# Shifting SBUF tiles with pads so that dense float32r operands start alike modulo 256 bytes, and returning a residual in two halves

## The chip, the cores and the metric

The kernel runs on one core of one Trainium2 chip. The metric is the device time in microseconds (us) of one launch; the time of a kernel is the median of its runs. The profile is one execution on the same core, taken by the hardware profiler. A product below is one TensorE matmul instruction.

## What is computed

The reference is two model blocks over 512 tokens of width 1024, in float32, with 256 tokens of context.

- The first block normalises the tokens, multiplies them by `w_in`, runs a retention mixer and an RWKV-7 scan (both directions), multiplies by `w_out`, adds the residual, and applies a mixture of 16 experts with 64 tokens each.
- The second block has two layers. Layer 0 mixes by three groups of dilated attention (all q, k, v from one normalised input), multiplies by `a_wo`, adds the result to its input `h` (the residual), and applies an MLP. Layer 1 mixes by a gated convolution and applies a second MLP:

```python
h = h + y
h = h + mlp_sq_relu(rms_norm_2(h, norm2[i]), mlp_w1[i], mlp_w2[i])   # square(relu(x @ w1)) @ w2
```

## The kernel before, in words

**Dense products.** Every large matrix product is made of float32r products. Both operands are split into a high and a low float32r part (`split`, L156 to L159), and three products add up in PSUM: high by high, low by high, high by low. There are four places that issue them, always with 128 rows of contraction, 128 output partitions and (but for the 256 context tokens) 512 columns:

- `tok_major` (L333 to L335): tokens stationary (`hHi`, `hLo`, `cHi`, `cLo`), weights moving (`w_hi`, `w_lo`): (6+6+4) blocks of 24, 384 products.
- `mm3` (L162 to L164) from `ch_major`: weights stationary, `hHi`/`hLo` moving: 24 calls of 24, 576 products, and 240 products of 256 columns on the context. The same line from `dense_b`: weights `whi`/`wlo` stationary, `y2Hi`/`y2Lo` moving, 3 times 704 = 2112 products (the first matrix of both MLPs and the convolution's input).
- L706 to L708 (`mh`, `ml` stationary, `w_hi`, `w_lo` moving) and L1326 to L1328 (`mix` stationary, `Wo` moving): 96 products each, the two halves of `w_out`.
- `dense_g` (L1822 to L1824): activations stationary, weights `whi`/`wlo` moving: 3 times 640 products on `yHi`/`yLo` (attention projections and `a_wo`), 3 times 512 on `aHi`/`aLo` (second matrix of both MLPs) and 3 times 64 on `gHi`/`gLo` (convolution's output).

Weights come by DMA from DRAM in 512 KB pieces on SyncE's (SP's) queue (`ahead`, L1794 on), in the order of the list `plan`, and ScalarE and VectorE split them one or two pieces ahead of use.

**Where tiles lie.** SBUF tiles come from pools that are stacked from the left end or the right end of each partition in the order in which the code opens them. No row of the profile shows an address; added up from the pools' sizes, the first bytes modulo 256 are: `w_hi`, `w_lo`, `Wo`, `whi`, `wlo`, `yHi`, `yLo`: 224. `hHi`, `hLo`, `cHi`, `cLo`: 192. `mix`: 128. `mh`, `ml`: 96. `y2Hi`, `y2Lo`, `aHi`, `aLo`, `gHi`, `gLo`: 0. Slices of 128 or 512 float32 columns keep the same remainder. For attention group 1 the value projection reads `yHi` with a stride of four columns (L2043, `yHi[:, k, b::4]`), so its slices begin at 224, 228, 232 and 236. So before the change the pair of operands is alike (224 and 224) in the products on `yHi`/`yLo`, and unlike in the other dense products.

Of plain float32 products, the attention's value product `po` (L2156, L2158) has `PPT` and `v` at 224 and 224; the scan's `cV` (L1082) has `uUV` and `uL` at 224 and 224; the scan's `cU` (L1094) has `cv` at 224 and `TT` at 128.

**Around the residual.** After the first block the residual `xres` ([128, 4, 1024] float32, 2 MB) is copied to DRAM (`sx`), and its two column halves, `raws[0]` and `raws[1]`, serve as buffers for the attention's projections. For each half of the heads (`hf`) and each group (`g`), `project` makes q in `raws[0]`, k in `raws[1]` and v; a generator `qk_T` normalises, rotates and transposes q or k in small steps, run between the steps of the next dense product by `drive` from the list `jobs`; `attend` is put in the same list. With `g == 2` v is made in `raws[0]`, stored to DRAM (`sV`, L2061, one DMA for each of four blocks) and loaded back in another order (L2068, four DMAs) into a tile of its own.

At the end of the last group (`hf` 1, `g` 2) the whole residual is loaded back by one DMA (L2260) on SP's queue, behind the loads of v. Then the first half of `a_wo`'s rows is multiplied (`dense_g` with `halves=(0, 1)`) while `jobs` still runs the last attention group and the merge of the groups: first output columns 0 to 511, then columns 512 to 1023. `add_res` adds each block's PSUM sum to `xres` on VectorE (L1856) and so frees the PSUM buffer; there are four accumulators.

Of the kernel before, what the change touches and what calls it, by code (L numbers as in the profile page):

```python
# [10 lines left out]
F32 = mybir.dt.float32  # L11
# [116 lines left out]
def _body(tc, nc, st, A, out, dbg, stop):  # L128
    V, ACT, PE, POOL = nc.vector, nc.scalar, nc.tensor, nc.gpsimd
    cst = st.enter_context(tc.tile_pool(name="cst", bufs=1))  # L130
    psp = [None]

    def ps(name="ps", tag="p"):
# [38 lines left out]
    pw = pa.enter_context(ExitStack())  # L172
    wr = pw.enter_context(tc.tile_pool(name="wr", bufs=4, side="right"))
    wh = pw.enter_context(tc.tile_pool(name="wh", bufs=3, side="right"))
    hp = pw.enter_context(tc.tile_pool(name="hp", bufs=1, side="right"))
    pr_ = pa.enter_context(ExitStack())
    M = pr_.enter_context(tc.tile_pool(name="M", bufs=10))
# [21 lines left out]
    xt, raws = [], {}  # L199
# [291 lines left out]
    for i in range(4):  # L491
        for d in range(2):
            b = i if d == 0 else 3 - i
# [63 lines left out]
    for pr in range(4):  # L557
        sg = []
        for d in range(2):
            a, _ = ch_major(1536 + 512 * d + pr * 128, False)  # L560
            t, g = med([128, S], name="gt"), med([128, S], name="sg")
# [18 lines left out]
    NT = S + CT  # L580
    p1 = pa.enter_context(ExitStack())
    P1 = p1.enter_context(tc.tile_pool(name="P1", bufs=1))
    W3 = p1.enter_context(tc.tile_pool(name="W3", bufs=1))

    def wide(name, tag="W3", bufs=3):
# [282 lines left out]
    ZX = xps.enter_context(tc.tile_pool(name="zX", bufs=3, side="right"))  # L868
    pools = {n: p2.enter_context(tc.tile_pool(name=n, bufs=4, side="right")) for n in ("uL11", "uKB", "uL12", "UP")}
    UP = pools["UP"]  # L870
    ZP, RP_, TP, LP = (p2.enter_context(tc.tile_pool(name=n, bufs=1)) for n in ("ZP", "RP", "TP", "LP"))
    mask = const("mask", nc.scalar, pool=ZP)
    anti = const("anti", nc.scalar, pool=ZP)
    epsg = ZP.tile([128, 1], F32, name="epsg")
# [855 lines left out]
    C1 = pc_.enter_context(tc.tile_pool(name="C1", bufs=1, side="right"))  # L1730
    WC = pc_.enter_context(tc.tile_pool(name="WC", bufs=3, side="right"))
    TC = pc_.enter_context(tc.tile_pool(name="TC", bufs=1))

    def tmp(shape, name, bufs, dt=F32):
        return TC.tile(shape, dt, tag=name, name=name, bufs=bufs)
# [40 lines left out]
    for l in range(2):  # L1776
        if l:
            for j in range(4):
                for i in (1, 2, 0):
                    plan += cols(Wb, i * 1024 + j * 256)  # L1780
        if l:
            for n in range(2):
                plan += rows(Wbo, 0, n * 512)
        else:
            r0, r1 = rows(Wo, 0, 0), rows(Wo, 0, 512)
            plan += r0[:2] + r1[:2] + r0[2:] + r1[2:]
        for qf in range(4):
            for j in range(4):
                plan += cols(W1[l], qf * 1024 + j * 256)
            for n in range(2):  # L1790
                plan += rows(W2[l], qf * 1024, n * 512)
# [19 lines left out]
    def dense_g(lhs, done, halves=(0, 1, 2, 3), before={}):  # L1811

        acc = [ps("acc", "a") for _ in range(4)]
        for half in halves:
            hi, lo = weights([128, 2, 512])
            if half in before:
                before[half]()
            for b in range(4):
                for kk in range(2):
                    k = half * 2 + kk  # L1820
                    xh, xl = lhs(k, b)
                    PE.matmul(acc[b], xh, hi[:, kk], start=k == 2 * halves[0], stop=False)  # L1822
                    PE.matmul(acc[b], xl, hi[:, kk], start=False, stop=False)  # L1823
                    PE.matmul(acc[b], xh, lo[:, kk], start=False, stop=k == 2 * halves[-1] + 1)  # L1824
                if half == halves[-1]:
                    done(b, acc[b])
                yield
# [19 lines left out]
    def nat(t):  # L1847
        return lambda k, b: (t[0][:, k, b * 128:(b + 1) * 128], t[1][:, k, b * 128:(b + 1) * 128])
# [112 lines left out]
    def qk_T(raw, dst, g, i):  # L1961

        sq_ = tmp([128, 4, 8], "qss", 2)
        for b in range(4):
            t = tmp([128, 512], "qsq", 2)
            ACT.activation(t, raw[:, b], AF.Square)
            V.tensor_reduce(sq_[:, b], t.rearrange("p (h d) -> p h d", d=64), axis=AX.X, op=OP.add)
            if b % 2:
                yield
        r = rsqrt(TC, sq_.rearrange("p b h -> p (b h)"), 32, EPS, 1.0 / 64)  # L1970
        yield

        def turn(b):
            x3 = raw[:, b].rearrange("p (h d) -> p h d", d=64)
            V.tensor_tensor(x3, x3, r[:, b * 8:b * 8 + 8, None].to_broadcast([128, 8, 64]), op=OP.mult)
            t = tmp([128, 8, 2, 8], "qrp", 2)
            xr = x3[:, :, 0:16].rearrange("p h (t d) -> p h t d", t=2)
            V.tensor_tensor(t, xr[:, :, ::-1], rt[:, g, i, b, 1].rearrange("p (t d) -> p t d", t=2)[:, None]
                            .to_broadcast([128, 8, 2, 8]), op=OP.mult)
            x16 = x3[:, :, 0:16]  # L1980
            V.tensor_tensor(x16, x16, rt[:, g, i, b, 0][:, None].to_broadcast([128, 8, 16]), op=OP.mult)
            V.tensor_tensor(x16, x16, t.rearrange("p h t d -> p h (t d)"), op=OP.add)

        def trans(b):
            pt = ps("pt", "t")
            for pr in range(4):
                PE.transpose(pt[:, pr * 128:(pr + 1) * 128], raw[:, b, pr * 128:(pr + 1) * 128], ident)  # L1987
            if g == 0:
                o, s_ = dst[:, :, b * 128:(b + 1) * 128], pt.rearrange("p (r t) -> p r t", r=4)
                ACT.activation(o, s_, AF.Copy, scale=gsc[:, g, i:i + 1])  # L1990
            else:
                ns = 4 if g == 1 else 16
                mm = 128 // ns
                for pr in range(4):
                    o = dst[:, pr].rearrange("p (s m) -> p m s", s=ns)[:, b * mm:(b + 1) * mm]
                    ACT.activation(o, pt[:, pr * 128:(pr + 1) * 128].rearrange("p (m s) -> p m s", s=ns), AF.Copy,
                                   scale=gsc[:, g, i:i + 1])

        for b in range(6):
            if b < 4:  # L2000
                turn(b)
            yield
            if b > 1:
                trans(b - 2)
                yield
# [3 lines left out]
    def drive(main, n=1):  # L2009

        for _ in main:
            for j in list(jobs):
                for _ in range(n):
                    if next(j, jobs) is jobs:
                        jobs.remove(j)
                        break

    def drain():
        while jobs:
            drive([0])  # L2020

    def project(hf, g):

        own = []
        dst = []
        for i in range(2):
            dst.append(AT.tile([128, 4, S], F32, name="qkT", tag=f"qk{i}", bufs=2))
            raw = raws[i]
            bf = {}
            if hf == g == i == 0:  # L2030
                bf = {0: lambda: turns(range(4), 0, y1), 1: lambda: (turns((4, 5), 0, y1), ranks()),
                      2: lambda: (turns((6, 7), 0, y1), tables())}
            drive(dense_g(nat(y1), qk_evac(raw), before=bf))
            for j in own:
                for _ in j:
                    pass
                if j in jobs:
                    jobs.remove(j)
            own = [qk_T(raw, dst[i], g, i)]
            jobs.extend(own)  # L2040
        lhs = nat((yHi, yLo))
        if g == 1:
            lhs = lambda k, b: (yHi[:, k, b::4], yLo[:, k, b::4])  # L2043
        if g == 2:
            v = raws[0]
        else:
            v = AT.tile([128, 4, 512], F32, name="v", tag="v")
        vx = None
        if g == 0:
            vx = AT.tile([128, 4, 512], F32, name="vx", tag="vx", bufs=1)  # L2050

        def done(b, acc):
            r = rr[g == 1][:, b:b + 1]
            ACT.activation(v[:, b], acc, AF.Copy, scale=r)
            if g == 0:
                if b:
                    V.tensor_scalar(vx[0:64, b - 1], acc[0:64], r[0:64], None, op0=OP.mult)
                if b < 3:
                    V.tensor_scalar(vx[64:128, b + 1], acc[64:128], r[64:128], None, op0=OP.mult)
            if g == 2:  # L2060
                nc.sync.dma_start(sV[hf, b * 128:(b + 1) * 128], v[:, b])  # L2061

        drive(dense_g(lhs, done))
        drain()
        if g == 2:
            v = AT.tile([128, 4, 512], F32, name="v", tag="v")
            for j in range(4):
                nc.sync.dma_start(v[:, j], sV[hf].rearrange("(m s) n -> s m n", s=16)[4 * j:4 * j + 4])  # L2068
        return dst[0], dst[1], v, vx

    def attend(g, O, md, qT, kT, v, vx):
# [185 lines left out]
            jobs.append(j)  # L2257
    for pr in range(4):
        split(yHi[:, pr], yLo[:, pr], oT0[:, pr])
    nc.sync.dma_start(xres, sx)  # L2260
    ss = sums()
    drive(dense_g(nat(y1), add_res(0), halves=(0, 1)), 4)
    drive(dense_g(nat(y1), add_res(1), halves=(0, 1)), 2)
    drain()
    at_.close()
    y2 = [pc_.enter_context(tc.tile_pool(name=n, bufs=1)).tile([128, 8, S], F32R, name=n) for n in ("y2Hi", "y2Lo")]
# [83 lines left out]
```

## Time and profile before

| | us |
|---|---|
| median of 3 runs | 2904.22 (2894.70 to 2904.94) |
| profiled execution, its own time | 2906.07 |
| span of its instructions | 2904.2 |
| TensorE busy | 2746.8 (95%) |
| VectorE busy | 1360.5 (47%) |
| ScalarE busy | 1024.9 (35%) |
| mean granted TensorE clock | 0.96 of full speed |

Matmuls are pipelined, and their ends are modelled: a row gives a product some 0.4 us, while the next one starts 0.23 us later. What a stream of products costs is therefore read from the distance of their starts. A row of busy time by stretch gives for each engine its busy time and, in brackets, its number of instructions, then TensorE's granted clock, the DMA engines' busy share and GB/s.

### The profile page before, as it was taken

What the parts mean: (1) busy time and instruction counts of PE and PEld (TensorE: products, weight loads), DVE (VectorE), ACT (ScalarE), POOL (GpSimd) and SP (SyncE); (2) the same over time, 40 slices, a digit from 0 to 9 for tenths busy, and PEclk for the clock granted to TensorE, in tenths of its full rate; (3) what the DMA queues carried; (4) which work ended last, traced back from release to release, by engine and by line L of the source; (5) the groups of instructions that cost most, each with busy time, mean ns of one, the idle gap of its engine ahead of it and who ended that gap; (6) DMA issues with size and microseconds to landing.
All of it is one profiled execution on the core that took longest, in us unless ns stands there. A gap on an engine that the chain in (4) does not pass through costs nothing.

```text
span 2904.2 us, 38123 instructions
## 1 busy us (share of the span) xinstructions
PE 2746.8 (95%) x15198; PEld 1951.0 (67%) x15198; DVE 1360.5 (47%) x2452; ACT 1024.9 (35%) x1988; POOL 268.2 (9%) x266
## 2 busy tenths in 40 slices
PE   7999997578899999979999999989999999999999
PEld 5767555457744444438688667857888888888887
DVE  4354286897621111236545654655344454444433
ACT  4232354356411111125446444634223332333223
POOL 1102045545100000011000000000000000000000
PEclk9999987789899999999999999988999999999999
DMA  6205755436779999983122211232222223222222
GB/s 246 81 22 170 232 176 164 145 105 168 268 283 409 408 409 409 409 307 121 51 63 91 70 59 59 66 109 66 94 94 94 94 89 94 94 93 95 93 93 92
DMA packets 253329, 456.33 MB, mean 157 GB/s; under 512 B 32367, under 2 KB 127160, under 8 KB 252640
## 3 DMA queue, kind: packets, MB, share of 16 engines
q1 hardware_dynamic: 236272, 438.44, 43.4%
q10 hardware_dynamic: 13632, 7.79, 0.9%
q0 software_dynamic: 3248, 7.67, 0.8%
q8 instruction: 120, 1.97, 0.3%
q14 instruction: 57, 0.47, 0.0%
HBM read 425.45 MB, written 28.40 MB: 156 GB/s over the span
## 4 chain that ended last, share of the span: by engine, by line
PE 72%; DVE 6%; DMA 3%; ACT 1%; issue 0%; POOL 0%; SPq 0%; DVEq 0%; ACTq 0%
PE pe L1555 11%; PE acc L1822 10%; PE acc L1824 10%; PE acc L1823 10%; PE accb L162 6%; PE accb L163 6%; PE accb L164 6%; PE pS L2104 2%; DVE zZ L973 2%; DVE zT L971 2%; DMA wexp<-in_w_down 1%; PE po L2156 1%; PE pt L1987 1%; PE pf L2233 1%; DMA xres<-sx 1%; PE pgat L1583 1%
## 5 line engine op out<-in xcount | busy, mean ns | idle before, releaser
L159 DVE TENSOR_TENSOR wlo<-wc,whi 128x1024 fp32r<-128x1024 f32 x238 | 291.4, 1224 | 483.0 <-ACT whi L158 468.5
L158 ACT CAST whi<-wc 128x1024 fp32r<-128x1024 f32 x240 | 251.8, 1050 | 499.3 <-PE acc L1823 313.7
L1822 PE MATMUL acc<-whi,yHi 128*128 128x512 f32 x640 | 274.9, 431 | 6.3 <-DVE xres L1856 5.9
L163 PE MATMUL accb<-y2Lo,whi 128*128 128x512 f32 x704 | 278.4, 395 | 0.0
L162 PE MATMUL accb<-y2Hi,whi 128*128 128x512 f32 x704 | 277.6, 395 | 0.1
L164 PE MATMUL accb<-y2Hi,wlo 128*128 128x512 f32 x704 | 277.5, 395 | 0.0
L1555 PE MATMUL pe<-wexp,xg 128*64 128x512 f32 x1008 | 263.7, 597 | 1.5 <-DMA wexp<-in_w_up 1.5
L1824 PE MATMUL acc<-wlo,yHi 128*128 128x512 f32 x640 | 258.8, 405 | 0.0
L1823 PE MATMUL acc<-whi,yLo 128*128 128x512 f32 x640 | 257.2, 402 | 0.0
L1822 PE MATMUL acc<-whi,aHi 128*128 128x512 f32 x512 | 202.7, 396 | 0.0
L1823 PE MATMUL acc<-whi,aLo 128*128 128x512 f32 x512 | 202.6, 396 | 0.0
L1824 PE MATMUL acc<-wlo,aHi 128*128 128x512 f32 x512 | 202.5, 396 | 0.0
L1555 PEld LDWEIGHTS pe<-wexp,xg 128*64 128x64 f32 x1008 | 89.2, 136 | 150.9 <-issue 144.9
L1822 PEld LDWEIGHTS acc<-whi,yHi 128*128 128x128 f32 x640 | 131.5, 206 | 43.8 <-issue 15.7
L163 PEld LDWEIGHTS accb<-y2Lo,whi 128*128 128x128 f32 x704 | 132.0, 187 | 32.6 <-DVE y2Lo L1749 0.5
L162 PEld LDWEIGHTS accb<-y2Hi,whi 128*128 128x128 f32 x704 | 131.9, 187 | 32.7 <-ACT whi L158 0.5
L164 PEld LDWEIGHTS accb<-y2Hi,wlo 128*128 128x128 f32 x704 | 132.0, 187 | 31.9
L1824 PEld LDWEIGHTS acc<-wlo,yHi 128*128 128x128 f32 x640 | 131.1, 205 | 28.9 <-issue 4.8
L1823 PEld LDWEIGHTS acc<-whi,yLo 128*128 128x128 f32 x640 | 132.2, 207 | 20.7 <-issue 1.4
L1823 PEld LDWEIGHTS acc<-whi,aLo 128*128 128x128 f32 x512 | 96.2, 188 | 23.3
L1822 PEld LDWEIGHTS acc<-whi,aHi 128*128 128x128 f32 x512 | 96.2, 188 | 23.2
L1824 PEld LDWEIGHTS acc<-wlo,aHi 128*128 128x128 f32 x512 | 96.2, 188 | 23.2
(656 smaller groups left out, 4645.1 us busy)
## 6 DMA issues: line engine op xcount, KB each, us to landing
wexp<-in_w_gate SPq DMA_DIRECT2D x64, 1024.0 KB
wc<-in_mlp_w SPq DMA_DIRECT2D x128, 512.0 KB
wexp<-in_w_up SPq DMA_DIRECT2D x62, 1024.0 KB
wexp<-in_w_down SPq DMA_DIRECT2D x62, 1024.0 KB
wc<-in_a_wqkv SPq DMA_DIRECT2D x72, 512.0 KB
wmod<-in_w_mod SPq DMA_DIRECT2D x32, 512.0 KB
w_b<-in_w_in SPq DMA_DIRECT2D x24, 512.0 KB
wc<-in_b_win SPq DMA_DIRECT2D x24, 512.0 KB
```

The costliest lines, as they stand in the source:

```text
L158: ACT.copy(hi, src)
L159: eng.tensor_tensor(lo, src, hi.bitcast(F32), op=OP.subtract)
L162: PE.matmul(o, whi, xhi, start=first, stop=False)
L163: PE.matmul(o, whi, xlo, start=False, stop=False)
L164: PE.matmul(o, wlo, xhi, start=False, stop=last)
L971: V.tensor_tensor(tm, Z[:, j + 1:, j:j + 1].to_broadcast([128, m, j]), Z[:, j:j + 1, :j].to_broadcast([128, m, j]), op=OP.mult)
L973: V.tensor_tensor(Z[:, j + 1:, :j], Z[:, j + 1:, :j], tm, op=OP.add)
L1555: PE.matmul(o[n][64 * e:64 * e + 64], lhs(k, e), w[e][:, kk, n * 512:n * 512 + 512], start=k == 0, stop=k == 7)
L1822: PE.matmul(acc[b], xh, hi[:, kk], start=k == 2 * halves[0], stop=False)
L1823: PE.matmul(acc[b], xl, hi[:, kk], start=False, stop=False)
L1824: PE.matmul(acc[b], xh, lo[:, kk], start=False, stop=k == 2 * halves[-1] + 1)
L2104: PE.matmul(pS[:, x * wd + lo:x * wd + hi], qT[r, pr, b * 128:(b + 1) * 128], kT[r, pr, ks], start=True, stop=True)
```

## The change

The change opens small pools that hold nothing but a pad (224, 128, 96 and 224 bytes per partition) at four places of the stack, so that tiles opened behind each pad move by that many bytes. On the right side `hHi`, `hLo`, `cHi`, `cLo` (with the other tiles of `hp`) go from 192 to 224. On the left `mh`, `ml` go from 96 to 224; `mix`, with the scan's tiles behind it (`TT` and others), from 128 to 224; everything that layer 0 and layer 1 open behind the pool `TC` goes up by 224, so `y2Hi`, `y2Lo`, `aHi`, `aLo`, `gHi`, `gLo` from 0 to 224, and the attention's `v` from 224 to 192. No instruction is added by a pad.

The residual comes back in eight DMAs of 256 KB in place of one of 2 MB: columns 512 to 1023 as soon as the last k has been transposed out of `raws[1]` (a generator `back(1)` chained to `qk_T`), columns 0 to 511 after the loads of v. The first half of `a_wo`'s rows is then multiplied in the other order of columns, 512 to 1023 first, and the list of weights follows.

```diff
+    def pad(stack, name, n, side="left"):
+
+        stack.enter_context(tc.tile_pool(name=name, bufs=1, side=side)).tile([128, n // 4], F32, name=name)
+
...
     wh = pw.enter_context(tc.tile_pool(name="wh", bufs=3, side="right"))
+    pad(pw, "padh", 224, "right")
     hp = pw.enter_context(tc.tile_pool(name="hp", bufs=1, side="right"))
...
     P1 = p1.enter_context(tc.tile_pool(name="P1", bufs=1))
+    pad(p1, "pad3", 128)
     W3 = p1.enter_context(tc.tile_pool(name="W3", bufs=1))
...
-    ZP, RP_, TP, LP = (p2.enter_context(tc.tile_pool(name=n, bufs=1)) for n in ("ZP", "RP", "TP", "LP"))
+    ZP = p2.enter_context(tc.tile_pool(name="ZP", bufs=1))
+    pad(p2, "padm", 96)
+    RP_, TP, LP = (p2.enter_context(tc.tile_pool(name=n, bufs=1)) for n in ("RP", "TP", "LP"))
...
     TC = pc_.enter_context(tc.tile_pool(name="TC", bufs=1))
+    pad(pc_, "padc", 224)
...
-            plan += r0[:2] + r1[:2] + r0[2:] + r1[2:]
+            plan += r1[:2] + r0[:2] + r0[2:] + r1[2:]
...
+    def back(n):
+        for b in range(4):
+            nc.sync.dma_start(raws[n][:, b], sx[:, b, n * 512:n * 512 + 512])
+        yield
...
             own = [qk_T(raw, dst[i], g, i)]
+            if hf and g == 2 and i:
+
+                own = [itertools.chain(own[0], back(1))]
             jobs.extend(own)
...
                 nc.sync.dma_start(v[:, j], sV[hf].rearrange("(m s) n -> s m n", s=16)[4 * j:4 * j + 4])
+            if hf:
+                for _ in back(0):
+                    pass
...
-    nc.sync.dma_start(xres, sx)
     ss = sums()
-    drive(dense_g(nat(y1), add_res(0), halves=(0, 1)), 4)
-    drive(dense_g(nat(y1), add_res(1), halves=(0, 1)), 2)
+    drive(dense_g(nat(y1), add_res(1), halves=(0, 1)), 4)
+    drive(dense_g(nat(y1), add_res(0), halves=(0, 1)), 2)
     drain()
```

## Rows read from the trace of the kernel before

**Rows 1.** The page, its first part: busy time of TensorE, share of span, instructions.

```profile
PE 2746.8 (95%) x15198; PEld 1951.0 (67%) x15198; DVE 1360.5 (47%) x2452; ACT 1024.9 (35%) x1988; POOL 268.2 (9%) x266
```

**Rows 2.** The chain of waits from 1976 us to the end, by line.

```profile
by line: PE accb L162 17.8%; PE accb L163 17.7%; PE accb L164 17.7%; PE acc L1823 15.1%; PE acc L1824 15.1%; PE acc L1822 15.0%; PE pt L1746 1.2%; PE prb L2299 0.1%; DVE xres L1858 0.1%; ACT qsq L1860 0.1%; issue 0.0%; ACTq L2346 0.0%; ACTq
```

**Rows 3.** Busy time by stretch: length, PE, PEld, DVE, ACT, POOL, clock, DMA, GB/s.

```profile
34.00:140.00 106.00, 104.20 (x536) 81.38 (x535) 46.17 (x83) 35.01 (x59) 12.38 (x9) 0.98 0.38 124
190.00:300.00 110.00, 108.58 (x515) 77.40 (x514) 44.42 (x63) 35.77 (x51) 22.90 (x24) 1.00 0.46 144
300.00:500.00 200.00, 179.83 (x689) 112.38 (x688) 125.59 (x121) 88.93 (x128) 68.95 (x49) 0.87 0.60 185
2040.00:2904.00 864.00, 860.15 (x3723) 691.64 (x3721) 364.01 (x437) 262.52 (x346) 0.00 (x0) 1.00 0.29 93
```

**Rows 4.** Timeline, TensorE, y2 by whi (0 and 224), 16 triples: start, duration.

```profile
2199.92 0.40 PE L162 MATMUL accb<-y2Hi,whi 128*128 128x512 f32 x1
...
2211.12 0.40 PE L162 MATMUL accb<-y2Hi,whi 128*128 128x512 f32 x1
```

**Rows 5.** Timeline, TensorE, whi by aHi (224 and 0), 7 triples.

```profile
2600.42 0.40 PE L1822 MATMUL acc<-whi,aHi 128*128 128x512 f32 x1
...
2605.32 0.40 PE L1822 MATMUL acc<-whi,aHi 128*128 128x512 f32 x1
```

**Rows 6.** Timeline, TensorE, hHi by w_hi (192 and 224), 14 triples.

```profile
224.10 0.39 PE L162 MATMUL acc<-hHi,w_hi 128*128 128x512 f32 x1
...
233.90 0.40 PE L162 MATMUL acc<-hHi,w_hi 128*128 128x512 f32 x1
```

**Rows 7.** Timeline, TensorE, whi by yHi (224 and 224), 15 triples.

```profile
1870.18 0.39 PE L1822 MATMUL acc<-whi,yHi 128*128 128x512 f32 x1
...
1880.38 0.39 PE L1822 MATMUL acc<-whi,yHi 128*128 128x512 f32 x1
```

**Rows 8.** Timeline, TensorE, whi by yHi with a stride of four columns, 7 triples.

```profile
1480.19 0.39 PE L1822 MATMUL acc<-whi,yHi 128*128 128x512 f32 x1
...
1485.12 0.40 PE L1822 MATMUL acc<-whi,yHi 128*128 128x512 f32 x1
```

**Rows 9.** Groups by line and shape: count, busy us, mean ns of one, idle before.

```profile
L1822 PE MATMUL acc<-whi,yHi 128*128 128x512 f32 x640 | 274.9, 431 | 6.3 <-DVE xres L1856 5.9 <-ACT yHi L1748 0.4
L1823 PE MATMUL acc<-whi,yLo 128*128 128x512 f32 x640 | 257.2, 402 | 0.0
L1822 PE MATMUL acc<-whi,aHi 128*128 128x512 f32 x512 | 202.7, 396 | 0.0
L1082 PE MATMUL cV<-uUV,uL 128*64 128x64 f32 x384 | 24.0, 243 | 23.6 <-ACT uUV L1072 17.3 <-DVE uUV L1074 6.0
L1094 PE MATMUL cU<-cv,TT 128*64 128x64 f32 x384 | 19.3, 239 | 0.0
```

**Rows 10.** The chain of waits, 1900 to 2050 us: start, us, what.

```profile
1901.52 20.30 DMA xres<-sx
```

**Rows 11.** Timeline around the residual; in brackets idle time and what ended it.

```profile
1904.80 1.79 PE L2156 MATMUL po<-diag,v 128*64 128x128 f32 x16 [1.99 <-DMA v<-sV]
1921.91 0.69 DVE L1856 TENSOR_TENSOR xres<-acc,xres 128x512 f32<-128x512 f32 x1 [5.83 <-DMA xres<-sx]
1922.66 0.79 PE L1822 MATMUL acc<-whi,yHi 128*128 128x512 f32 x1 [5.91 <-DVE xres L1856]
1939.07 0.69 DVE L1856 TENSOR_TENSOR xres<-acc,xres 128x512 f32<-128x512 f32 x1 [0.49 <-PE acc L1824]
```

**Rows 12.** Busy time by stretch around the residual, columns as in rows 3.

```profile
1922.00:1930.00 8.00, 7.34 (x58) 4.54 (x59) 5.86 (x14) 2.40 (x17) 0.00 (x0) 0.57 0.01 3
```

**Rows 13.** Timeline, SP's queue: storing v and loading it back.

```profile
1893.42 3.77 SPq L2061 DMA_DIRECT2D sV<-xres  x3
1899.01 2.47 SPq L2068 DMA_DIRECT2D v<-sV  x4
```

**Rows 14.** DMA view, 1900 to 2050 us: GB/s in 40 slices of 3.75 us.

```profile
GB/s 126 260 245 194 108 86 1 0 146 0 140 2 139 1 0 0 0 0 0 4 140 0 137 23 120 9 131 144 0 29 129 122 140 35 111 140 44 96 140 39
```

## The prediction

> **What bounds the kernel now.** I read the page's first part, the chain of waits, the busy time by stretch and then the timeline of single products. TensorE is busy for 95% of the span [rows 1]. From 1976 us to the end the chain of waits is nearly nothing but dense products of L162 to L164 and L1822 to L1824 [rows 2], and from 2040 to 2904 us TensorE is busy for 860.15 of 864 us at a granted clock of 1.00, with VectorE at 364, ScalarE at 263 and the DMA engines at 0.29 [rows 3]. So in the last 30% of the kernel the time is the number of products times the distance of their starts, and nothing else is near. The same holds early on: 104.20 of 106 us from 34 to 140 us, 108.58 of 110 from 190 to 300; from 300 to 500 us TensorE still has 179.83 of 200, at a clock of 0.87 [rows 3].
>
> The distance of starts is what the pads can touch, and the trace holds products of both kinds. A triple is three products on the same operands. With y2 by whi (0 and 224 modulo 256) 16 triples take 2211.12 - 2199.92 = 11.20 us, so 48 products are 233.3 ns apart [rows 4]. With whi by aHi (224 and 0) 21 products take 4.90 us: 233.3 ns [rows 5]. With hHi by w_hi (192 and 224) 42 take 9.80 us: 233.3 ns [rows 6]. With whi by yHi (224 and 224), on the very line and weights of the aHi products, 45 products take 1880.38 - 1870.18 = 10.20 us: **226.7 ns** [rows 7]. With a stride of four columns in yHi 21 products take 4.93 us, 234.8 ns [rows 8]: three of four slices are unlike there, and the stride is a second difference. All five stretches are free of other work, and one product lasts 0.39 or 0.40 us in each, so the clock is the same. The one difference between rows 5 and rows 7 that the code shows is where the tile begins. 6.6 ns of 233.3 is 2.8%.
>
> The Trainium skill (TensorE: Matmul & The Clock Gate, "Step-by-step: what each phase is for") speaks against this reading: TensorE has two separate SBUF read ports, and loading the next tile's weights takes no read bandwidth from the running matmul. By that rule the relative start of two operands would not matter, and the first rival below would be the outcome. The trace disagrees so far, with 226.7 against 233.3 ns. The same page gives some 216 ns for the distance of warm products of 512 columns, which neither kind reaches here.
>
> **The change, part by part.** The sum is made against the profiled execution's own 2906.07 us (span 2904.2 and 1.87 around it); the median of the runs, 2904.22, is 1.85 lower.
>
> *padc.* It turns y2, a and g from 0 to 224, so 2112 + 1536 + 192 = 3840 products become alike. All lie after 1976 us, where TensorE is the whole chain [rows 2, 3]. At 233.3 - 226.7 = 6.6 ns each that is 25.3 us. Bounds: nothing, if the start is not the cause; 25.3 us if every product reaches 226.7 (no stretch shows less). I take 25.3, since these products run in long streams as those of rows 7 do, but with one reserve that is a rival below: in rows 7 the tokens are stationary and the weights move, while in the 2112 products on y2 it is the other way round.
>
> *padh, pad3, padm.* 576 + 384 + 96 + 96 = 1152 products of 512 columns become alike; at 6.6 ns each, 7.6 us. TensorE bounds the first stretches and less so the third [rows 3], and short bursts between other work may not settle at 226.7. I take two thirds, 5 us; the ends are 0 and 7.6.
>
> *Plain float32 products.* padc makes `po` unlike (v goes to 192, PPT stays at 224), padm makes `cU` alike. In the scan a group that is alike (`cV`, 243 ns) and one that is not (`cU`, 239 ns) [rows 9] show no price either way, so I take nothing. Bounds: if 6.6 ns held here too, the 256 products of `po`, two instructions each, would lose 3.4 us and the 384 instructions of `cU` would gain 2.5.
>
> *The residual.* The load of 2 MB is issued at 1901.52 us and takes 20.30 us on the chain [rows 10]. VectorE stands 5.83 us for it and TensorE, which needs the accumulators, 5.91 us [rows 11]. After that pause the granted clock is 0.57 for 8 us [rows 12], between its levels of 1.2 and 2.4 GHz; against the full clock that is 0.43 x 8 = 3.4 us. Removed: up to 9.3 us.
>
> Added are seven DMA issues on SP's queue. The three stores of v there take 3.77 us in all, most of it waiting for v's blocks, and the four loads of v 2.47 us, 0.6 each [rows 13]. `back(1)` falls behind the second store, so its four issues (some 2.5 us by the loads' price) lie in those waits; behind them in the queue stand the last two stores, the weights' next piece and the loads of v, and for those waits the value product of the last group, which already stands 1.99 us for v [rows 11]. Its 1 MB also lies ahead of v on the DMA engines: at the 245 to 260 GB/s of the busiest slices [rows 14] that is an estimated 4 us. So v comes 0 to 4.3 us later, in part at a lower clock. I take 2 us, because the stores leave the engines idle for part of that time, and keep 0 and 5 as ends.
>
> `back(0)` stands behind the loads of v, in the place of the old load, with half its bytes. It is wanted only after the first 48 products on columns 512 to 1023 and the attention steps between them; before, the second set of additions began at 1939.07 us, 17.2 us after the first [rows 11], and its data would even at the old load's 20.30 us be there at about 1922 us. It is hidden; if the last rings were as late as that and the stage had come forward by 9 us, it would still not be waited for. Behind it on SP's queue is one piece of weights, which is not wanted before those additions. The swapped order of columns costs nothing, as the list of weights is swapped with it. When the stall is gone, the next late thing is the serial chain of the merge, which the change leaves alone.
>
> Residual in all: 9.3 - 2 = about 7 us, ends 4 and 9.
>
> **Sum:** 25.3 + 5 + 7 = 37.3 us; 2906.07 - 37.3 = 2868.8, and 1.85 less as the median stands: **2867 us**, 1.3% faster.
>
> **Rivals.**
>
> 1. *The start does not matter.* The 226.7 ns would come from something else in the projections, as where yHi lies as a whole. For it: only one tile pair shows the short distance. Against it: rows 5 and 7 share line, shape, weights and clock. Then only the residual counts: 2906.07 - 7 - 1.85 = 2897 us, no change that can be told. Chance 0.10. (The skill's rule on the two ports gives this time.) That the pads do not reach 224 would look the same, but the sums of bytes leave no doubt: 0 + 224, 96 + 128, 128 + 96, and 192 - 224 = 224 modulo 256.
>
> 2. *Only products with the tokens stationary gain.* The 2112 on y2 and the 576 on hHi stay at 233.3. Then 1728 x 6.6 = 11.4 us, 2 us of the token mixer and 7 of the residual: 20.4 us, so 2884 us, 0.7% faster. For it: no pair with moving tokens that is alike stands in the trace. Against it: unlike pairs cost 233.3 ns both ways round [rows 4, 5]. Chance 0.10.
>
> 3. *Alike is the dear kind, and the kernel slows.* For it: the groups' mean for one product is 402 ns on yLo against 396 on aHi, and 431 on yHi [rows 9]. If that were the cost of being alike, 3840 products would lose 6 ns each, 23 us; less the residual's 7 that is 16 us more, 2920 us. It decides from 1.8 ns a product on. Against it: ends are modelled, the groups on yHi mix in stretches of low clock and breaks by attention work, and the clean starts say the opposite [rows 7]. Chance 0.05.
>
> **How the numbers follow.** My forecast has the remaining 0.75. About 0.5% (14.5 us) is what a measurement of this kernel can tell from no change; the runs of before alone spread by 10 us. Forecast and rival 2 are faster by more than that: 0.85. Rival 1 is the same: 0.10. Rival 3 is slower: 0.05. For the range, the low end takes 25.3 + 7.6 + 9 and 2.5 of `cU`: 44 us, 2860, and I go to 2858; the high end takes in rival 2 with the residual's lower end, 2887. Rivals 1 and 3 are left out.
>
> **What would show it.** Right: in the second MLP a triple takes 0.680 us in place of 0.700, and the stretch that took 864 us takes some 840; the triples on hHi take 0.680 as well; L1856 waits for no DMA, and the clock stays up around 1920 us. Wrong: triples still 0.700 us (rival 1); 0.680 on L1822 to L1824 but 0.700 on L162 to L164 (rival 2); longer ones (rival 3); a wait of the value product for v well over 2 us, which would eat the residual's part; or a new limit in the MLPs, visible as idle time of TensorE on the split of weights.

## The result and the profile after

| | before | after |
|---|---|---|
| median | 2899.46 us (4 runs, 2891.11 to 2904.94) | 2866.03 us (4 runs, 2860.30 to 2868.56) |
| profiled execution: own time, span | 2906.07, 2904.2 us | 2863.71, 2861.6 us |
| mean granted clock | 0.960 | 0.962 |

The ratio is **0.9884 [0.9851, 0.9918]**: 1.2% faster. Where it went is read from five landmarks, the first starts of named products in the two profiled executions:

| stretch, us | before | after | difference |
|---|---|---|---|
| start to the first expert product | 815.9 | 808.3 | -7.6 |
| experts, to the first attention projection | 489.1 | 489.1 | 0 |
| attention and merge, to the first product on y2 | 688.5 | 678.7 | -9.8 |
| first MLP, to the first product on gHi | 499.5 | 485.8 | -13.7 |
| the rest (convolution, second MLP) | 411.2 | 399.8 | -11.4 |

So 25.1 of 42.6 us come from the last two rows, which only the pads can touch. The page's first part, TensorE (answers to rows 1), and the busy time of the last stretch, which is shifted by 17.4 us so that it holds the same work as the last of rows 3:

```profile
PE 2710.8 (95%) x15198; PEld 1948.4 (68%) x15198; DVE 1358.0 (47%) x2452; ACT 1025.2 (36%) x1988; POOL 269.5 (9%) x266
```

```profile
2022.60:2861.60 839.00, 835.16 (x3718) 691.04 (x3716) 363.05 (x436) 261.85 (x346) 0.00 (x0) 1.00 0.30 96
```

The number of instructions and the clock of 1.00 are as before (3718 records against 3723), VectorE's and ScalarE's work is the same, and TensorE is idle for under 4 of the 839 us. The same products stand closer together. The timeline of TensorE in the kernel after shows by how much; each pair of rows is the first and the last start of an unbroken stretch, of 540 products on y2, 189 on aHi and 42 on hHi (answers to rows 4 to 6):

```profile
2338.73 0.39 PE L167 MATMUL accb<-y2Hi,whi 128*128 128x512 f32 x1
...
2461.16 0.39 PE L167 MATMUL accb<-y2Hi,whi 128*128 128x512 f32 x1
...
2640.03 0.39 PE L1832 MATMUL acc<-whi,aHi 128*128 128x512 f32 x1
...
2682.87 0.39 PE L1832 MATMUL acc<-whi,aHi 128*128 128x512 f32 x1
...
210.81 0.40 PE L167 MATMUL acc<-hHi,w_hi 128*128 128x512 f32 x1
...
220.36 0.39 PE L167 MATMUL acc<-hHi,w_hi 128*128 128x512 f32 x1
```

(2461.16 - 2338.73) / 540 = 226.7 ns, (2682.87 - 2640.03) / 189 = 226.7, (220.36 - 210.81) / 42 = 227.4; before they were 233.3 each. The groups by line and shape say it more faintly (answers to rows 9), because a product's end is modelled:

```profile
L1832 PE MATMUL acc<-whi,yHi 128*128 128x512 f32 x640 | 272.7, 428 | 0.4 <-ACT yHi L1758 0.4
L1832 PE MATMUL acc<-whi,aHi 128*128 128x512 f32 x512 | 199.4, 389 | 0.0
L1103 PE MATMUL cU<-cv,TT 128*64 128x64 f32 x384 | 18.5, 233 | 0.1
```

aHi falls from 396 to 389 ns. The group on yHi, whose tiles the change did not touch, keeps its duration (431 and 428), but the 6.3 us of idle time in front of it, 5.9 of them for the residual, are gone.

The second part of the change shows in SP's queue (answers to rows 13), with the columns start, time to the last issue of the row, and count:

```profile
1874.09 3.55 SPq L2034 DMA_DIRECT2D xres<-sx  x2
...
1880.50 3.53 SPq L2034 DMA_DIRECT2D xres<-sx  x2
1884.08 0.43 SPq L2079 DMA_DIRECT2D sV<-xres  x1
...
1887.61 0.45 SPq L2034 DMA_DIRECT2D xres<-sx  x1
...
1889.69 0.89 SPq L2034 DMA_DIRECT2D xres<-sx  x2
...
1892.03 4.24 SPq L2086 DMA_DIRECT2D v<-sV  x4
1896.31 2.42 SPq L2034 DMA_DIRECT2D xres<-sx  x1
```

Four loads of the residual are issued before the first store of v and three more before the loads of v; only the last stands behind those, where the code puts four. No addition of the residual waits for a DMA any more. What is late next is v: the view of the tile `po` lists the waits of the value product, and the busy time by stretch gives the clock behind that wait and in an earlier stretch of the attention.

```profile
L2177 PE MATMUL po<-diag,v x64: 272/273/476, 1899.8 to 1923.3; 128*64 128x128 f32 x64
its engine sat idle before it (us, times) until:
  DMA v<-sV: 3.0, 1
```

```profile
1652.40:1666.10 13.70, 13.70 (x31) 7.78 (x30) 7.90 (x15) 1.04 (x1) 0.00 (x0) 0.51 0.12 39
1901.00:1909.00 8.00, 8.00 (x89) 4.87 (x91) 4.26 (x13) 2.21 (x12) 0.00 (x0) 0.57 0.40 126
```

TensorE waits 3.0 us where it waited 1.99 [rows 11], and then runs at 0.57 for 8 us, mostly at its lower level of 1.2 GHz. Before, it ran at the lower level for 3.4 us behind the wait for v and for 10.2 us behind the wait for the residual [rows 12]; now for 6.8 us, once.

### The profile page after: what moved, and what is told of

Its sections match the earlier page's. It is cut to its first block, busy times and chain, and to the rows that moved or that the text cites. A ratio compares the mean times of both kernels' runs of the same rounds, so it can differ in the third digit from the quotient of the medians.

```text
span 2861.6 us, 38144 instructions
## 1 busy us (share of the span) xinstructions
PE 2710.8 (95%) x15198; PEld 1948.4 (68%) x15198; DVE 1358.0 (47%) x2452; ACT 1025.2 (36%) x1988; POOL 269.5 (9%) x266
## 4 chain that ended last, share of the span: by engine, by line
PE 72%; DVE 6%; DMA 3%; ACT 1%; issue 0%; POOL 0%; SPq 0%; DVEq 0%; ACTq 0%
PE pe L1564 11%; PE acc L1832 10%; PE acc L1834 10%; PE acc L1833 10%; PE accb L167 6%; PE accb L168 6%; PE accb L169 6%; PE pS L2125 2%; DVE zT L980 2%; DVE zZ L982 2%; DMA wexp<-in_w_down 1%; PE po L2177 1%; PE pt L1997 1%; PE pf L2254 1%; PE pgat L1592 1%; PE pT L2154 1%
## 5 line engine op out<-in xcount | busy, mean ns | idle before, releaser
L163 ACT CAST whi<-wc 128x1024 fp32r<-128x1024 f32 x240 | 252.2, 1051 | 474.7 <-PE acc L1833 299.8
L1833 PEld LDWEIGHTS acc<-whi,yLo 128*128 128x128 f32 x640 | 131.0, 205 | 20.5 <-issue 1.3
```

Of the source, the lines that this page charges most:

```text
L163: ACT.copy(hi, src)
```

## The experiments

Four questions: does each half of the change give what the sum says; is it the relative start of the operands that counts, and how exactly; what made the residual early; and what the next late thing is worth.

**The halves alone.** Three kernels on one chip, in runs by turns with the kernel before (21 runs): the changed kernel (5), the pads alone (6), and the residual alone (10). The edit for the pads alone, against the changed kernel:

```diff
-            if hf and g == 2 and i:
-                own = [itertools.chain(own[0], back(1))]
...
-            if hf:
-                for _ in back(0):
-                    pass
...
+    nc.sync.dma_start(xres, sx)
-    drive(dense_g(nat(y1), add_res(1), halves=(0, 1)), 4)
-    drive(dense_g(nat(y1), add_res(0), halves=(0, 1)), 2)
+    drive(dense_g(nat(y1), add_res(0), halves=(0, 1)), 4)
+    drive(dense_g(nat(y1), add_res(1), halves=(0, 1)), 2)
```

The residual alone leaves out the four lines `pad(pw, "padh", ...)`, `pad(p1, "pad3", ...)`, `pad(p2, "padm", ...)` and `pad(pc_, "padc", ...)`.

> The changed kernel itself, as a yardstick on the same chip for its two parts. If the parts are independent, its gain is the sum of the gains of the next two runs: some 33 us off the kernel before (1.2%), 25 us of it after the first product on y2.

> Only the pads; the residual returns in one load at the old place. If the common start is the cause: every dense triple outside the attention falls from 0.700 to 0.680 us, the stretch from the first product on y2 to the end shortens by 25 us (911 to 886), the stretch up to the first expert product by 5 to 8 us, and the wait of L1856 for the residual (5.8 us) stays: about 32 us faster. If the start did nothing and the whole gain were the residual's: no change that can be told.

> Only the residual's return in halves, no pads. My theory: the wait of 5.8 us and the 10 us at the low clock behind it go, the value product waits 1 us longer for v, so 7 to 10 us between the first attention product and the first product on y2; triples in the MLP stay at 0.700 us. Rival: the low clock only comes at another place, and the gain is no more than the 5.9 us of TensorE's pause.

| | median, us | ratio to before (2897.18) | y2 to the end, us |
|---|---|---|---|
| both | 2864.32 | 0.9878 [0.9858, 0.9897] | 885.5 |
| pads | 2866.87 | 0.9897 [0.9877, 0.9917] | 885.6 |
| residual | 2890.24 | 0.9974 [0.9958, 0.9989] | 910.5 |

The parts add up: 1.03% + 0.26% = 1.29%, against 1.22%. The stretch from the first product on y2 to the end takes 910.7 us in the kernel before; the pads bring it to 885.6, the residual leaves it alone. The residual is worth 0.0026 x 2897 = 7.5 us (3 to 12 by its interval), or 5.5 by the difference of the first two runs. With the pads alone the stall is where it was; the timeline of VectorE and the chain of waits of that run:

```profile
1910.72 0.69 DVE L1866 TENSOR_TENSOR xres<-acc,xres 128x512 f32<-128x512 f32 x1 [4.63 <-DMA xres<-sx]
```

```profile
1890.56 20.06 DMA xres<-sx
```

In the residual's own run the wait for v and the lower clock behind it grew; the timeline of TensorE shows the value product:

```profile
1902.43 1.97 PE L2173 MATMUL po<-diag,v 128*64 128x128 f32 x16 [4.14 <-DMA v<-sV]
```

Here the clock stands at the lower level from 1901.1 to 1911.4 us. So the rival named for this run, that the low clock only comes at another place and no more than 5.9 us is gained, holds in its first half for this execution, and a gain of 3 to 12 us does not rule out the second.

One more thing is read from these runs. In 11 of the 14 profiled executions the clock falls to the lower level for 13.7 us (17.1 in one) some 355 us into the attention; in the residual's run it does not (same stretch, counted from the first projection):

```profile
1659.80:1673.50 13.70, 13.59 (x58) 8.65 (x57) 12.45 (x27) 1.93 (x3) 0.00 (x0) 1.00 0.14 39
```

Nothing in the code differs there. From the first product of the first merge (`pf`, some 347 us into the attention) to the start of the wait for v, the three executions without it take 246.4 us, and five that have it and also load the residual in eight take 252.2 or 252.3. So such a stretch is worth some 6 us, and it comes and goes between executions; the stretch at the merge is another (30.7 us in the profiled execution of before, 23.9 in two others, 17.1 to 20.5 in the rest, among them the pads alone). Of the 9.8 us between projections and y2, then, the 4.7 in the merge can't be put down to the change, and one profile can't settle a question of 5 us about this part of the kernel; medians of many runs can.

**The relative start.** Three kernels with other pads follow, each run once; the one run of before beside them took 2904.24 us. First, whole multiples of 32 bytes off:

```diff
-    pad(pc_, "padc", 224)
+    pad(pc_, "padc", 32)
...
+        pad(pm_, f"pada{i}", (32, 128)[i])
...
+    pad(cv_, "padg", 64)
```

> Pads changed so that the activations stand otherwise to the weights (which stay at 224 modulo 256): y2 64 bytes on, a of the first MLP 96, g 128, a of the second MLP 192. If only equality modulo 256 helps, all four are 0.700 us a triple and the end is 25 us later than in the changed kernel. If a smaller modulus were enough (64 or 128), y2, g and the second a stay at 0.680 us. If the kernel before merely stood at a bad distance of 32 bytes, all four are at 0.680 us or below.

2873.35 us, span 2871.2. The timeline of TensorE in this run, stretches of 540 products on y2 (start of activation less start of weight: 64 modulo 256), 189 on aHi in the first MLP (96) and 141 on gHi (128):

```profile
2342.71 0.39 PE L167 MATMUL accb<-y2Hi,whi 128*128 128x512 f32 x1
...
2466.31 0.39 PE L167 MATMUL accb<-y2Hi,whi 128*128 128x512 f32 x1
...
2018.69 0.39 PE L1832 MATMUL acc<-whi,aHi 128*128 128x512 f32 x1
...
2062.96 0.40 PE L1832 MATMUL acc<-whi,aHi 128*128 128x512 f32 x1
...
2467.00 0.39 PE L1832 MATMUL acc<-whi,gHi 128*128 128x512 f32 x1
...
2499.76 0.39 PE L1832 MATMUL acc<-whi,gHi 128*128 128x512 f32 x1
```

228.9, 234.2 and 232.3 ns; aHi in the second MLP (192) stands at 228.8. So the price is graded: differences of 64 and 192 cost 2.2 ns a product, 128 some 5.6, 96 and the 32 of before 6.6 to 7.5. None of the three outcomes named ahead of the run came out. The stretch from y2 to the end takes 898.6 us, 13.1 longer than with equal starts (885.5) and 12.1 shorter than before: a price that is all or nothing would have given the whole 25. Then, small differences:

```diff
+        pad(pm_, f"pada{i}", 192)
...
+            o = (1, 8)[i]
+            aHi, aLo = (AP_.tile([128, 8 * S + 64], F32R, name=n)[:, o:o + 8 * S].rearrange("p (k n) -> p k n", k=8)
+                        for n in ("aHi", "aLo"))
...
+    y2 = [pc_.enter_context(tc.tile_pool(name=n, bufs=1)).tile([128, 8 * S + 8], F32R, name=n)[:, 4:4 + 8 * S]
+          .rearrange("p (k n) -> p k n", k=8) for n in ("y2Hi", "y2Lo")]
...
+    pad(cv_, "padg", 192)
```

> How exact the common start must be, with unit stride: y2Hi 16 bytes on, y2Lo 48, a of the first MLP 4, a of the second MLP 32, g 0. If any difference costs, only g stays at 0.680 us a triple. If what counts is a block of 32 bytes or more, the first a (4 bytes) and the products on y2Hi (16) stay at 226.7 ns; then the stride, not the start, is what makes the projections of group 1 dear.

2869.96 us, span 2867.9. Timeline of TensorE, 189 products on aHi in the first MLP, which lies one float (4 bytes) off, and 189 in the second, eight floats (32 bytes) off:

```profile
2011.70 0.39 PE L1832 MATMUL acc<-whi,aHi 128*128 128x512 f32 x1
...
2055.61 0.39 PE L1832 MATMUL acc<-whi,aHi 128*128 128x512 f32 x1
...
2640.78 0.40 PE L1832 MATMUL acc<-whi,aHi 128*128 128x512 f32 x1
...
2684.88 0.40 PE L1832 MATMUL acc<-whi,aHi 128*128 128x512 f32 x1
```

232.3 and 233.3 ns: four bytes cost nearly the whole price. y2 (16 bytes off for the high part, 48 for the low) gives 230.0 in its stretch of 540, and gHi, again at no difference, 227.0. Last, the place itself: weights and activations of the MLPs all go to 192, while yHi stays at 224.

```diff
+    pad(pc_, "padw", 32, "right")
...
-    pad(pc_, "padc", 224)
+    pad(pc_, "padc", 192)
```

> The weights of the second block moved to 192 modulo 256, y2, a and g to 192 as well, yHi and yLo left at 224. If the relation of the two operands counts: MLP triples stay at 0.680 us though all addresses are new, and the clean stretches of the attention's projections on yHi rise from 0.680 to 0.700 us, which makes the stretch from the first attention product to the first product on y2 some 5 us longer. If the place 224 itself counts: the MLPs go to 0.700 us and the projections stay.

2870.11 us, span 2868.0. Timeline of TensorE, 540 products on y2 (192 and 192) and 87 of the projections (192 and 224):

```profile
2345.18 0.39 PE L167 MATMUL accb<-y2Hi,whi 128*128 128x512 f32 x1
...
2467.60 0.39 PE L167 MATMUL accb<-y2Hi,whi 128*128 128x512 f32 x1
...
1314.88 0.39 PE L1834 MATMUL acc<-whi,yLo 128*128 128x512 f32 x1
...
1335.17 0.39 PE L1834 MATMUL acc<-whi,yLo 128*128 128x512 f32 x1
```

226.7 at another common place, and 233.2 for the projections that were the short ones before. The same operands change sides as their starts do: it is the relation that counts and neither the place, nor the tile, nor the line. The stretch from y2 to the end takes 885.5 us as with the pads at 224, and the attention from its first projection to the first merge takes 350.1 us, where the other executions have 347.1 to 348.0.

**What made the residual early.** The kernel before, with nothing but eight plain loads in the place of the one:

```diff
-    nc.sync.dma_start(xres, sx)
+    for n in range(2):
+        for b in range(4):
+            nc.sync.dma_start(raws[n][:, b], sx[:, b, n * 512:n * 512 + 512])
```

> The kernel before with the residual's one load replaced by eight loads of 256 KB at the same late place, first half of the columns first, order of products unchanged. If the early issue is what helps, little changes: the first addition still waits, by 5.8 us or somewhat less. If the form of the load is (one transfer in pieces of 16 KB, whose last part sits on few queues behind v), the wait of L1856 falls below 2 us here as well, and 5 us or more are gained without moving anything ahead of v.

2891.48 us, 0.9975 [0.9959, 0.9991]: the gain of the residual's own run (0.9974), without `back()` and without the swapped columns. They were meant to be late here and were not. SP's queue in this run:

```profile
1878.65 3.54 SPq L2262 DMA_DIRECT2D xres<-sx  x2
...
1885.06 3.52 SPq L2262 DMA_DIRECT2D xres<-sx  x2
1888.63 0.43 SPq L2061 DMA_DIRECT2D sV<-xres  x1
...
1896.86 2.43 SPq L2068 DMA_DIRECT2D v<-sV  x4
1899.34 2.30 SPq L2262 DMA_DIRECT2D xres<-sx  x1
```

The loads stand behind everything in the code, yet the queue holds them in the order of the changed kernel. In these programs the order of DMA issues follows when the block under each load becomes free, and not the line on which it is written; one load of the whole tile is free only with the last block, eight are free one by one. To tell time from form, the one late load was kept, with the copy in DRAM laid out so that it moves in shorter packets:

```diff
-    sx = dr.tile([128, 4, D], F32, name="sx")
+    sx = dr.tile([4, 128, D], F32, name="sx").rearrange("b p d -> p b d")
```

> The kernel before, with the residual's place in DRAM laid out as [4, 128, D] rather than [128, 4, D], so that the one load of 2 MB moves in packets of 4 KB rather than 16 KB; when it is issued does not change (about 1901 us). If what made the residual late was its place in the queue, behind the loads of v, the vector engine still stands 4 to 6 us for it and the run is within 2 us of before. If it was the form, a few long packets queued on a few rings, the wait is below 2 us and the granted clock does not fall around 1920 us.

2905.58 us in its one run, beside a median of 2899.70 for before (2897.63 to 2905.34): no faster, though 5.9 us off where at most 2 had been expected. Its chain of waits and its timeline of VectorE:

```profile
1903.00 21.18 DMA xres<-sx
```

```profile
1924.27 0.69 DVE L1856 TENSOR_TENSOR xres<-acc,xres 128x512 f32<-128x512 f32 x1 [4.10 <-DMA xres<-sx]
```

With packets of 4 KB the load takes 21.18 us in place of 20.30, and VectorE waits 4.10 us for it, against 5.83 in before and 4.63 in the pads' run: the size of the packets is not what makes it late. Being issued behind v need not be the whole of it either. Two rows of busy time by stretch (the last two numbers are the DMA engines' busy share and GB/s) and one of the DMA view, all of the kernel before, show how the load ends; the last row belongs to the second stretch:

```profile
1903.00:1912.00 9.00, 7.20 (x65) 5.28 (x66) 3.84 (x11) 3.42 (x21) 0.00 (x0) 0.81 0.97 241
1916.00:1920.00 4.00, 0.75 (x14) 0.30 (x2) 0.08 (x1) 1.09 (x2) 0.00 (x0) 0.84 0.24 101
DMA packets 30, 0.40 MB, mean 101 GB/s; under 512 B 1, under 2 KB 1, under 8 KB 6
```

While v and the residual come together, nearly all engines are busy. The residual's last packets (24 of the 30 have 8 KB or more, and only its packets are so long here) then come at a quarter of the engines, the same share that v has when it comes alone (below). This fits the rival named ahead of this run and of the one with eight loads: v holds four engines longer than the rest, and the residual's pieces on those four come last. On this reading the load is late because it stands behind v, and behind a v that lies on few engines; eight loads issued behind v were not run, and how much each part is worth stays open. Both halves in their simplest form, the four pads and the plain loop:

> The four pads and, for the residual, a plain loop of eight loads where the one load stood: no back(), no other order of the columns. If the order of DMA issues follows from when each is ready and not from where it is written, this is the whole of the change: ratio 0.988 as for the changed kernel (0.9878), 2862 to 2868 us. If back() between the stores is worth something by itself, it is 3 us or more later.

2863.29 us (2860.52 to 2875.48), 0.9889 [0.9871, 0.9908]: the changed kernel's gain. `back()` and the new order of columns add nothing that five rounds show.

**The next late thing.** v comes back by four loads, each of which gathers from a view whose slowest dimension counts four. The view of the DMA engines in the changed kernel, 1885 to 1935 us in 40 slices of 1.25 us, busy share in tenths and GB/s:

```profile
DMA  7998976752259932221100004600000182000048
GB/s 272 406 387 275 303 265 198 287 182 100 102 167 272 264 115 98 98 95 57 36 0 0 0 0 184 236 7 13 0 0 0 13 297 110 0 0 7 0 101 311
```

Around slices 10, 11 and 15 to 18, when little but v is left, the share is 0.2 at some 100 GB/s, where the same engines moved up to 406. The Trainium skill (DMA: Bandwidth & Descriptors, "Rules for kernel authors") has the rule for it: a transfer uses at most as many of the 16 engines as its slowest dimension counts. A digit of 2 (0.2 to 0.3) agrees with four of 16. So v was loaded by sixteen DMAs of 32 partitions:

```diff
             for j in range(4):
-                nc.sync.dma_start(v[:, j], sV[hf].rearrange("(m s) n -> s m n", s=16)[4 * j:4 * j + 4])
+                for s in range(4):
+                    nc.sync.dma_start(v[32 * s:32 * s + 32, j], sV[hf].rearrange("(m s) n -> s m n", s=16)[4 * j + s])
```

First on the plain loop, then, with the changed kernel beside it on another chip, on the changed kernel:

> As the run with the plain loop, and v comes back by sixteen loads of 32 partitions in place of four of 128. If the four loads are slow because they lie on few rings, the last group's value product waits 1 us or less for v in place of 3.0, the clock does not fall behind it, and the run is 3 to 6 us faster than the plain loop. If the path is the stores of v and the issues themselves, sixteen issues of 0.4 to 0.6 us in place of four delay the last load, the wait is as long or up to 4 us longer, and the run is the same or slower.

> The changed kernel itself, with v loaded back by sixteen loads of 32 partitions in place of four. The run with the plain loop and sixteen loads took 2858.5 us, the one with four 2863.3, while their profiled executions were level (spans 2859.0 and 2858.4). If the wait for v is on the path, it is gone here and the run is 3 to 5 us faster than the changed kernel beside it, in all its runs. If the merge behind it takes the time back, as in the profiled execution (43.1 in place of 41.0 us from the merge's first product to the second MLP), the two are within 2 us of each other.

> The changed kernel, unaltered, on the same chip as the run with sixteen loads of v: 2862 to 2868 us as in the runs so far, the value product of the last group waiting 2.4 to 4.1 us for v and the granted clock falling behind it in some executions only.

| | median, us | ratio to before |
|---|---|---|
| plain loop, v in 16 | 2858.49 (beside 2863.29 with v in 4) | 0.9850 [0.9834, 0.9867] |
| changed kernel, v in 16 | 2855.80 | 0.9847 [0.9827, 0.9867] |
| changed kernel | 2863.23 | 0.9876 [0.9855, 0.9897] |

4.8 us in the first pair and 7.4 in the second, on two chips (3 to 6 and 3 to 5 had been expected). Five of the six runs with sixteen loads took 2853.49 to 2857.07 us; the sixth, which is the profiled one, took 2869.74 and had lost its time long before the attention (first expert product at 820.6 us; 814.1 in the changed kernel beside it and 808.3 in that of the result). Its stretch from the attention to the merge took 631.5 us against 637.5 in the changed kernel beside it. The views of `po`, of SP's queue and of the busy time in this run:

```profile
L2178 PE MATMUL po<-diag,v x64: 272/273/323, 1912.3 to 1930.3; 128*64 128x128 f32 x64
its engine sat idle before it (us, times) until:
  DVE diag L2145: 0.7, 2
```

```profile
1904.66 8.93 SPq L2087 DMA_DIRECT2D v<-sV  x16
```

```profile
1908.00:1916.00 8.00, 7.38 (x103) 5.12 (x101) 6.13 (x17) 3.42 (x21) 0.00 (x0) 1.00 0.58 157
1916.00:1930.00 14.00, 13.34 (x175) 9.19 (x175) 9.91 (x33) 8.32 (x42) 0.00 (x0) 1.00 0.20 76
```

No wait for v, and the clock is 1.00 all through. Sixteen issues take 8.93 us of SP's queue in place of 4.24, and nobody waits for that: a piece lands some 3.3 us after its issue, so the first are there while the last are being issued. This is the fastest version of the study; it beats the changed kernel by 0.3%. The two intervals of the second pair overlap a little, those of the first do not ([0.9834, 0.9867] against [0.9871, 0.9908]).

## Why the prediction was right

The forecast was 2867 us, and the median is 2866.03.

- **padc.** 3840 products by 6.6 ns, 25.3 us forecast; 25.1 measured in the profiled executions, and 25.1 with the pads alone (910.7 - 885.6). Clean streams of all three kinds stand at 226.7, those on y2 too, where the weights are stationary and the tokens move, which rows 7 had not shown. The reserve for them was not needed.
- **padh, pad3, padm.** 5 us forecast between 0 and 7.6. The first expert product moved by 7.6 us in the two profiles shown; over the profiled executions of this study it starts at 815.4 us on average in the four without these pads and at 809.8 in the ten with them, 5.6 us earlier. Within each set the starts spread by 5 and by 16 us, so this says no more than the size. The distances of starts say it better: at the full clock and in unbroken streams these products come 3.5 to 6.1 ns sooner in the profile after, 6.3 us in all.
- **Plain float32 products.** Taken at nothing. `cU` falls from 239 ns to 233 after padm, but takes 235 in the executions without it as well (residual alone, eight loads, short packets), and its distances of starts are alike (31.7 and 31.8 ns on average). `po`, which padc made unlike, keeps its mean of 285 ns (256 instructions) and its distance of 53.2. No price either way.
- **Residual.** 7 us forecast between 4 and 9; 7.5 and 7.2 by rounds in the two runs that have it alone, 5.5 as the difference of both and pads. The profiled executions agree: with the lower-clock stretch of 13.7 us in the attention, from the first product of the first merge to that of the second, they take 295.0 us on average in the three with the one load and 288.6 in the five with eight loads and v in four, 6.5 us less. The clock's share of the removed time, 3.4 us, was of the right size: of the 10.2 us at the lower level TensorE worked for 6.3, which costs some 3.1. The 2 us set against the gain are not borne out as a term of their own. In the two profiles shown the value product waits 1.0 us longer for v; over the executions it waits 2.0 to 3.1 us in the three with the one load and 2.1 to 4.1 in the nine with eight.

One step failed, without harm to the sum: "`back(1)` falls behind the second store" and "`back(0)` stands behind the loads of v". It took the order of the queue from the order of the code. SP's queue shows four loads in the 10 us ahead of the first store, and only one behind v; the argument that `back(1)`'s issues hide in the waits for the stores fell away, and the part of the change that reorders the code does nothing by itself. The sum survived since the loads came earlier than was assumed, not later; in this step that was luck. A sentence beside the sum failed too: the next late thing was not the merge but the load of v, and loading v otherwise gained 4.8 and 7.4 us.

Rival 1 (the start does not matter, 2897 us) falls by the pads alone, 0.9897, and by the projections, which become long when only their place is changed. The Trainium skill's rule that stood beside it (TensorE: Matmul & The Clock Gate, "Step-by-step: what each phase is for": two read ports, so loading weights takes nothing from the running product) would have all pairs alike; 226.7 against 232.3 ns for one float of difference disagrees. Whether it is the reading of the operands that collides was not tried; the runs show only that the time follows their difference. Rival 2 (only one way round gains, 2884) falls by 226.7 on y2 and aHi both. Rival 3 (alike is dear, 2920) falls by the same rows; the means of 402 against 396 on which it rested come from modelled ends, as it said itself.

The executions of plain loops and of `back()` differ by 3 to 4 us between attention and merge (634.2 and 633.7 against 637.3 to 637.5 three times) while their rounds do not. The traces put this down to v: the wait for it, with half of the time that TensorE works at the lower clock right behind it, comes to 2.4 us in each of the first two and to 5.4, 6.0 and 6.4 in the other three. Why the clock falls in one execution and not in another stays open. So does whether loading v by sixteen DMAs would alone cure the late residual of before: the quarter share at the end of its load speaks for it, and it was not tried.

## What to carry to other kernels

Where TensorE is the whole chain of float32r products of 512 columns, compare the distances of starts between pairs of operands in clean stretches: if two kinds differ on the same line, look at where the tiles begin, and pad until both begin alike modulo 256 bytes; 4 bytes of difference already cost most of the 2.8%. Here a load that covers a whole tile waited for the tile's last reader; cut along the tile's blocks, it went out piece by piece, and no code had to be moved for it. And where the DMA engines' busy share sits at a quarter with one load left, look at the dimension along which that load is cut: here it counted four, and other loads that shared the engines ended late with it.

## What had not been expected

The price of an unlike start is graded and not a matter of lines that do or don't share a boundary: in ns a product 226.7 at 0, 228.9 at 64, 228.8 at 192, 232.3 at 128, 232.3 at 4, 233.3 at 32, 234.2 at 96. A difference of 256 bytes is free: whi and aHi begin 256 apart modulo 512, whi and yHi at 0, and both stand at 226.7. With float32r products of 256 columns it is, if anything, the other way: 240 of them, on cHi and cLo, stand 118.4 ns apart when unlike and 119.7 when alike, 0.3 us in all. And a late wait can cost more than it lasts: behind the 5.83 us for the residual the clock stood at 1.2 GHz for 10.2 us, of which TensorE worked for 6.3, so some 3.1 us were lost besides; behind the 3.0 us for v in the changed kernel it stood there for 6.8 us, all of them worked, some 3.4 us lost. The length of the wait does not settle it: behind 2.0 us for v in before it fell for 3.4 us and behind 2.1 us in the run with whole multiples of 32 bytes for 6.8, but behind 2.4 us in the plain loop, and with v in sixteen, it stayed at 2.4 GHz.
